# Branch gates and branch projections with tokens in rows, in a one-core hybrid layer in fp32

## The chip, the core and the metric

The kernel runs on one of the eight cores of a Trainium2 chip. The metric is the device time of one execution in microseconds (us), the median of several runs. The profile is one execution taken by the hardware profiler. Its engines: PE (TensorE, matmuls), PEld (its weight loads, which overlap PE), DVE (VectorE), ACT (ScalarE), POOL (GpSimd) and SP, whose queue issues most transfers.

## The reference, cut to what matters

One layer with 256 tokens of width 2048 (`D_MODEL`), all in fp32, and a final norm. Four branches of width 1024 (block attention A, convolution C, sparse attention S, attention into a memory M) are made from one projection of the normalised tokens:

```python
xn = rms_norm(x, ln_g)
(a_q, a_k, a_v, a_g, c_b, c_c, c_h, c_g, s_q, s_k, s_v, s_g, m_q, m_g,
 i_q, i_k, i_w, r_a, r_c, r_s, r_m) = [xn @ w for w in cols]
...                                     # y_a, y_c, y_s, y_m: [256, 1024] each, times silu of its gate
mem_n = rms_norm(mem, mem_ln_g)         # 256 memory tokens
mk, mv = jnp.split(mem_n @ w_mem_kv, 2, axis=-1)
...
merged = (jax.nn.sigmoid(r_a) * (y_a @ w_branch[0]) + jax.nn.sigmoid(r_c) * (y_c @ w_branch[1])
          + jax.nn.sigmoid(r_s) * (y_s @ w_branch[2]) + jax.nn.sigmoid(r_m) * (y_m @ w_branch[3]))
return rms_norm(x + merged @ w_out, final_g)
```

The branch gates r_a to r_m are 2048 wide each, 2048 inputs to a column; the branch products have 1024 inputs and 2048 columns.

## The kernel before, in words

**Products in parts.** Every fp32 operand of a large product is split exactly into hi and lo of 12 bits (`split`, L90 to L92: a cast on ACT, a subtraction on DVE), and three of the four partial products are summed in PSUM. Weights come from HBM in tiles "raw" of 1 MB, from a ring of three slots (L50) that `square_sums` (L168) and `load_mem` (L440) use too; `split_weights` (L101) splits each tile in two halves of 128x1024 into a ring of four (L51). A half is 2.8 us of PE's work.

**Two forms.** `project_t` (L127) makes the result transposed, columns on partitions: the weights are stationary, and for each chunk of 128 inputs and 128 columns there is one matmul with hi against the 2 x 256 columns of the tokens' hi and lo (L124, 512 columns) and one with lo against the tokens' hi (L125, 256). Its two halves are added by `sum_t` (L137: a copy on ACT, an addition on DVE) and scaled by 1/rms of each token, a row (`x_row`). `project` (L143) makes it with tokens in rows: the tokens are stationary, three matmuls of 512 columns (L161 to L163) for each half of the tokens.

**Where each is used.** Transposed: all q, k and gates of the branches (sections M_Q, M_G, S_Q, ... of 1024 columns), the branch gates (`gates`, L370, eight blocks of 256 columns for each branch, sigmoid at L378) and the branch products (`merge`, L381), which multiplies by the sigmoids and adds to `merged`, transposed too. In rows: the values (`to_values`, L213) and the output projection (L530), whose stationary operand is `mt`, the parts of `merged`; mt takes the place of x_hl, the parts of x (L508).

**Order.** M_Q (its first 512 columns while x arrives, L400), squares of x and x_row (L433 to L436), M_G with `load_mem` 0 to 3 hooked in after its four blocks (memT twice, mem twice, L452), w_mem_k, w_mem_v, memory attention, the indexer's projections, gates and products of M; then for S and A: q, k, values, gate section, attention over 8 heads (`masked_attention`, L248), gates, products; then C, and the output projection. x itself stays unnormalised in x_hl. Each engine works through its list in order; the lists are laid out by a planner that gives an instruction that comes earlier in the program the first turn and lets later ones pass when it isn't ready, so attention runs with the gates' matmuls in between. PSUM has eight banks: two tiles of two banks for projections, two for scores, one each for pp (transposed probabilities) and yp (L55 to L57).

Of the kernel before, what the change touches and what calls it, by code (L numbers as in the profile page):

```python
# [8 lines left out]
F32 = mybir.dt.float32  # L9
# [5 lines left out]
P = 128  # L15
# [17 lines left out]
# the columns of w_in that are projected transposed, in blocks of TB, and the place of each section's first block  # L33
SECTIONS = [(c, W) for c in (A_Q, A_K, A_G, C_B, C_C, C_H, C_G, S_Q, S_K, S_G, M_Q, M_G)] + [(R_0, 4 * D)]
# [3 lines left out]
BR_A, BR_C, BR_S, BR_M = 0, 1, 2, 3  # L38
TOPK = 64
# [3 lines left out]
def hybrid_kernel(ctx, tc, x, xT, mem, memT, ln_g, mem_ln_g, w_t, w_v, w_idx, conv_w, conv_b, w_mem_k, w_mem_v,  # L43
# [26 lines left out]
    # the tensor engine's clock and the activation table are ready when the first operands arrive  # L70
# [5 lines left out]
    wp = ps_1.tile([P, 512], F32, name="pp", tag="pp")  # L76
# [4 lines left out]
    # additive causal mask: columns 0:128 for queries 0..127, 128:384 for queries 128..255  # L81
# [19 lines left out]
    def split_weights(src, w):  # L101
        """(hi, lo, k) of each chunk k of the weights src [P, chunks, columns], in tiles w wide."""
# [11 lines left out]
    def split_tokens(raw, k, g, dst):  # L114
        """dst = (hi, lo) of raw * g."""
# [6 lines left out]
    def products_t(o, hi, lo, k, nk, act):  # L122
        """o[:, 0] + o[:, 1] gains chunk k of nk for the columns in hi, lo."""
        nc.tensor.matmul(o, lhsT=hi, rhs=act(k), start=(k == 0), stop=False)  # L124
        nc.tensor.matmul(o[:, 1], lhsT=lo, rhs=act(k)[:, 0], start=False, stop=(k == nk - 1))  # L125

    def project_t(src, act):  # L127
        """(a @ src)^T, at most TB columns: chunk j of 128 columns is acc[:, j, 0] + acc[:, j, 1]."""
        acc = ps_acc.tile([P, 2, 2, T], F32, name="acc", tag="acc")
        nk, c = src.shape[1:]  # L130
        for hi, lo, k in split_weights(src, TB):
            for j, c0 in enumerate(range(0, c, P)):
                c1 = min(c0 + P, c)
                products_t(acc[:c1 - c0, j], hi[:, c0:c1], lo[:, c0:c1], k, nk, act)
        return acc

    def sum_t(dst, acc, n=2, rows=P):  # L137
        """dst = both parts of project_t's result"""
        low = tmp.tile([P, 2, T], F32, name="low")
        nc.scalar.copy(out=low[:rows, :n], in_=acc[:rows, :n, 1])  # L140
        nc.vector.tensor_add(dst, acc[:rows, :n, 0], low[:rows, :n])

    def project(src, act, t_outer=False):  # L143
        """a @ src: acc[:, t, :c] for the tokens of half t."""
        nk, c = src.shape[1:]
        if t_outer:
            acc = [ps_s.tile([P, NB], F32, name=f"acc{t}", tag="s") for t in range(2)]
        else:
            both = ps_acc.tile([P, 2, NB], F32, name="acc", tag="acc")
            acc = [both[:, t] for t in range(2)]  # L150
        parts = split_weights(src, c)
        if t_outer:
            parts = list(parts)
            steps = ((p, t) for t in range(2) for p in parts)
        else:
            steps = ((p, t) for p in parts for t in range(2))
        for (hi, lo, k), t in steps:
            ts = slice(t * P, (t + 1) * P)
# [432 lines left out]
```

## Time and profile before

| | us |
|---|---|
| time, median of 3 runs | 1422.41 (1422.35 to 1422.84) |
| span of the profiled execution, first to last instruction | 1420.6 |
| PE busy | 1411.7 (99%) |
| PEld busy | 1223.6 (86%) |
| DVE busy | 902.0 (63%) |
| ACT busy | 724.5 (51%) |

The span leaves out what lies before the first and after the last instruction, 1.8 us against the median. Busy times are read with care: matmuls are pipelined and a matmul's busy time overlaps its neighbour's, so that a busy PE says only that it had something in work. Mean granted clock of the core: 0.998 of full speed.

### The profile page before, as it was taken

Reading aid. Unit: us, or ns where it says so; the run is one execution under the profiler, and the core shown is the slowest. Engines: PE = TensorE matmul, PEld = TensorE weight load, DVE = VectorE, ACT = ScalarE, POOL = GpSimd, SP = SyncE. Lnnn points to the kernel's source line nnn. Section 1 sums busy time; section 2 is a strip of 40 time slices with the busy share of each in tenths; the row PEclk is TensorE's granted clock in tenths of the full one; section 3 lists DMA queues with packets and bytes.
Section 4 is the critical chain, followed back from the end, with each engine's and each line's share of the span. In section 5 each row is a group of like instructions: output and inputs, shape, how many; then the busy total and the mean of one; then the engine's idle time right before and its main releaser. Section 6 shows DMA issues by size and latency. Waiting matters only on the chain.

```text
span 1420.6 us, 19646 instructions
## 1 busy us (share of the span) xinstructions
PE 1411.7 (99%) x7904; PEld 1223.6 (86%) x7904; DVE 902.0 (63%) x1169; ACT 724.5 (51%) x964; POOL 10.7 (1%) x25
## 2 busy tenths in 40 slices
PE   9999999999999999999999999999999999999997
PEld 8888888888888888888888888888888888888887
DVE  7755566658755558757655557857657656557754
ACT  7664356544444348744444347844444445445543
POOL 1000000000000000000000000000000000000000
PEclk9999999999999999999999999999999999999999
DMA  9775554555555554455555555455555666555552
GB/s 316 281 268 195 187 164 153 171 185 178 178 186 200 180 188 165 150 180 189 194 178 185 201 178 177 149 179 181 187 196 178 214 224 213 182 189 195 178 198 99
DMA packets 49963, 269.38 MB, mean 190 GB/s; under 512 B 6656, under 2 KB 17456, under 8 KB 19024
## 3 DMA queue, kind: packets, MB, share of 16 engines
q1 hardware_dynamic: 48960, 264.03, 54.7%
q0 software_dynamic: 624, 3.31, 0.6%
q8 instruction: 62, 1.02, 0.3%
q10 hardware_dynamic: 288, 0.79, 0.1%
q14 instruction: 29, 0.24, 0.0%
HBM read 265.88 MB, written 2.10 MB: 189 GB/s over the span
## 4 chain that ended last, share of the span: by engine, by line
PE 99%; issue 0%; DMA 0%; DVE 0%; ACT 0%; POOLq 0%; POOL 0%; DVEq 0%; SPq 0%; ACTq 0%
PE acc L124 53%; PE acc L125 27%; PE acc L163 5%; PE acc L162 5%; PE acc L161 5%; PE first L124 1%; PE pp L269 0%; PE s L242 0%; PE yp L242 0%; PE first L125 0%; PE yp L241 0%; PE s L241 0%; PE s L240 0%; PE yp L240 0%; PE s L254 0%
## 5 line engine op out<-in xcount | busy, mean ns | idle before, releaser
L124 PE MATMUL acc<-x_hl,hi 128*128 128x512 f32 x2576 | 917.5, 398 | 0.1
L92 DVE TENSOR_TENSOR lo<-raw,hi 128x1024 fp32r<-128x1024 f32 (+1 forms) x496 | 595.1, 1201 | 471.9 <-ACT hi L91 469.7
L91 ACT CAST hi<-raw 128x1024 fp32r<-128x1024 f32 (+1 forms) x496 | 511.1, 1031 | 655.4 <-PE acc L124 491.4
L125 PE MATMUL acc<-x_hl,lo 128*128 128x256 f32 x2576 | 725.4, 282 | 0.0
L124 PEld LDWEIGHTS acc<-x_hl,hi 128*128 128x128 f32 x2576 | 483.7, 188 | 114.9 <-DVE x_hl L118 0.8
L125 PEld LDWEIGHTS acc<-x_hl,lo 128*128 128x128 f32 x2576 | 483.1, 188 | 1.5
L124 PE MATMUL acc<-y,hi 128*128 128x512 f32 x512 | 181.2, 399 | 0.0
L125 PE MATMUL acc<-y,lo 128*128 128x256 f32 x512 | 143.7, 281 | 0.0
L124 PEld LDWEIGHTS acc<-y,hi 128*128 128x128 f32 x512 | 96.2, 188 | 23.6
L125 PEld LDWEIGHTS acc<-y,lo 128*128 128x128 f32 x512 | 96.7, 189 | 0.1
L140 ACT COPY low<-acc 128x512 f32<-128x512 f32 (+1 forms) x117 | 67.6, 578 | 0.3 <-PE acc L125 0.3
L161 PE MATMUL acc<-hi,mt 128*128 128x512 f32 (+1 forms) x160 | 55.5, 348 | 0.0
L163 PE MATMUL acc<-hi,mt 128*128 128x512 f32 (+1 forms) x160 | 55.3, 347 | 0.0
L162 PE MATMUL acc<-lo,mt 128*128 128x512 f32 (+1 forms) x160 | 55.0, 345 | 0.0
L163 PE MATMUL acc<-hi,x_hl 128*128 128x512 f32 x128 | 50.4, 394 | 0.0
L162 PE MATMUL acc<-lo,x_hl 128*128 128x512 f32 x128 | 50.2, 392 | 0.0
L161 PE MATMUL acc<-hi,x_hl 128*128 128x512 f32 x128 | 49.7, 388 | 0.0
L163 PEld LDWEIGHTS acc<-hi,mt 128*128 128x128 f32 x160 | 29.9, 187 | 4.2
L162 PEld LDWEIGHTS acc<-lo,mt 128*128 128x128 f32 x160 | 30.0, 188 | 4.0
L161 PEld LDWEIGHTS acc<-hi,mt 128*128 128x128 f32 x160 | 30.0, 188 | 3.6
L162 PEld LDWEIGHTS acc<-lo,x_hl 128*128 128x128 f32 x128 | 24.0, 188 | 5.5
L161 PEld LDWEIGHTS acc<-hi,x_hl 128*128 128x128 f32 x128 | 24.0, 188 | 5.4
(182 smaller groups left out, 980.4 us busy)
## 6 DMA issues: line engine op xcount, KB each, us to landing
raw<-in_w_t SPq DMA_DIRECT2D x156, 1024.0 KB, 5.2
raw<-in_w_branch SPq DMA_DIRECT2D x32, 1024.0 KB, 4.8
raw<-in_w_v SPq DMA_DIRECT2D x16, 1024.0 KB, 4.7
raw<-in_w_out SPq DMA_DIRECT2D x16, 1024.0 KB, 4.7
raw<-in_w_mem_k SPq DMA_DIRECT2D x8, 1024.0 KB, 5.1
raw<-in_w_mem_v SPq DMA_DIRECT2D x8, 1024.0 KB, 4.8
raw<-in_w_t SPq DMA_DIRECT2D x16, 256.0 KB, 5.8
raw<-in_x SPq DMA_DIRECT2D x2, 1024.0 KB, 4.8
```

Of the source, the lines that this page charges most:

```text
L91: nc.scalar.copy(out=hi, in_=src)
L92: nc.vector.tensor_sub(out=lo, in0=src, in1=hi.bitcast(F32))
L124: nc.tensor.matmul(o, lhsT=hi, rhs=act(k), start=(k == 0), stop=False)
L125: nc.tensor.matmul(o[:, 1], lhsT=lo, rhs=act(k)[:, 0], start=False, stop=(k == nk - 1))
L140: nc.scalar.copy(out=low[:rows, :n], in_=acc[:rows, :n, 1])
L161: nc.tensor.matmul(o, lhsT=ah, rhs=hi, start=(k == 0), stop=False)
L162: nc.tensor.matmul(o, lhsT=ah, rhs=lo, start=False, stop=False)
L163: nc.tensor.matmul(o, lhsT=al, rhs=hi, start=False, stop=(k == nk - 1))
```

## The change

Six things, all in one edit:

- The branch gates and the branch products are made in rows. `merge_branch` takes half of a branch's 2048 columns at a time: gates of two blocks of 512 columns (`project` with two sources in turn, four chunks each), sigmoid straight from PSUM, then the products of the same two blocks from y, times the sigmoids, added to merged. The order of one branch is gates, products, gates, products. The weights in HBM are laid out to suit.
- `merged` lies with tokens in rows. After the last branch `parts_of` transposes it on PE, 4 chunks x 2 token halves for each block of 512, into banks pp, and splits into mt.
- The tokens are normalised once: `normalize(b)`, hooked in after the four blocks of w_mem_k, adds the parts of four chunks of x_hl, multiplies by x_row and splits them back in place, through a tile xn from the ring raw. The later scalings by x_row or x_col go; M_Q and the memory's keys and values keep theirs.
- M_G moves behind the memory's values; `load_mem` moves ahead: 0 and 1 into the last two blocks of M_Q, 2 and 3 behind the squares of x.
- One ring of eight PSUM banks takes the place of the three pools.
- `sum_t` works bank by bank, 256 columns at a time.

```diff
-    ps_acc = ctx.enter_context(tc.tile_pool(name="ps_acc", bufs=2, space=PS))
-    ps_s = ctx.enter_context(tc.tile_pool(name="ps_s", bufs=2, space=PS))
-    ps_1 = ctx.enter_context(tc.tile_pool(name="ps_1", bufs=1, space=PS))
+    banks = ctx.enter_context(tc.tile_pool(name="banks", bufs=8, space=PS))
+    def bank(name):
+        return banks.tile([P, NB], F32, name=name, tag="b")
...
+    def sum_t(dst, acc, row=None, rows=P):
+        for j, a in enumerate(acc):
+            low = tmp.tile([P, T], F32, name="low")
+            nc.scalar.copy(out=low[:rows], in_=a[:rows, 1])
+            nc.vector.tensor_add(dst[:, j], a[:rows, 0], low[:rows])
+            if row is not None:
+                nc.vector.tensor_mul(dst[:, j], dst[:, j], row[:rows])
...
+    def project(srcs, act, name, t_outer=False):
+        nk = srcs[0].shape[1]
+        acc = [[bank(name)[:, :src.shape[2]] for src in srcs] for t in range(2)]
+        parts = [split_weights(src, src.shape[2]) for src in srcs]
...
+            steps = ((p, t, n) for k0 in range(0, nk, 4) for n in range(len(srcs))
+                     for p in itertools.islice(parts[n], 4) for t in range(2))
+        for (hi, lo, k), t, n in steps:
+            a = act(k)[:, :, t * P:(t + 1) * P]
+            products(acc[t][n], a[:, 0], a[:, 1], hi, lo, k == 0, k == nk - 1)
...
-    def gates(b):
-        sig = big.tile([P, KC, T], F32, name="sig", tag="m16b")
-        for j in range(8):
-            acc = project_t(w_t[FIRST[R_0] + 8 * b + j], x_act)
-            s = sig[:, 2 * j:2 * j + 2]
-            sum_t(s, acc)
-            nc.vector.tensor_mul(s, s, rows(x_row, 2))
-            nc.scalar.activation(out=s, in_=s, func=AF.Sigmoid)
-        return sig
...
+    def merge_branch(b, y, after=None):
...
+        for j in range(2):
+            blocks = (2 * j, 2 * j + 1)
+            sig = big.tile([P, 2, W], F32, name="sig", tag="m16b")
+            acc = project([w_n[GATES + 4 * b + n] for n in blocks], x_act, "r")
+            for t in range(2):
+                for n in range(2):
+                    nc.scalar.activation(out=sig[:, t, n * NB:(n + 1) * NB], in_=acc[t][n], func=AF.Sigmoid)
+            acc = project([w_branch[b, n] for n in blocks], lambda k: y[:, k], "w")
+            for n in range(2):
+                for t in range(2):
+                    m = merged[:, t, blocks[n] * NB:(blocks[n] + 1) * NB]
+                    g = sig[:, t, n * NB:(n + 1) * NB]
+                    if first:
+                        nc.vector.tensor_mul(m, acc[t][n], g)
+                    else:
+                        nc.vector.tensor_mul(g, acc[t][n], g)
+                        nc.vector.tensor_add(m, m, g)
+                if after is not None:
+                    after(blocks[n], merged)
...
+    for b in range(2, 4):
+        acc = project_t(w_sec(M_Q)[b], x_act)
+        load_mem(b - 2)
+        sum_t(q[:, 2 * b:2 * b + 2], acc)
+    for t in range(2):
+        square_sums(x, t, x_ss)
+    x_col, x_row = inv_rms(x_ss, "x")
+    nc.vector.tensor_mul(q, q, rows(x_row, 8))
+    for b in (2, 3):
+        load_mem(b)
     m_col, m_row = inv_rms(m_ss, "m")
+    def normalize(b):
+        ks = slice(4 * b, 4 * b + 4)
+        xn = rawp.tile([P, 4 * NB], F32, name="xn", tag="raw")[:, :4 * T].rearrange("p (k t) -> p k t", t=T)
+        nc.vector.tensor_add(xn, x_hl[:, ks, 0].bitcast(F32), x_hl[:, ks, 1].bitcast(F32))
+        nc.vector.tensor_mul(xn, xn, rows(x_row, 4))
+        split(x_hl[:, ks, 0], x_hl[:, ks, 1], xn)
+    k = to_heads("kt", w_mem_k, m_act, m_row, normalize)
+    v = to_values([w_mem_v[0], w_mem_v[1]], m_act, m_col)
+    gt = to_gate(M_G)
     y = memory_attention(q, k, v, gt)
     idx = indexer_parts()
-    sig = gates(BR_M)
-    merge(BR_M, sig, y)
+    merge_branch(BR_M, y)
...
+    def parts_of(n, merged):
+        for c in range(4 * n, 4 * n + 4, 2):
+            pp = halves(bank("pp"))
+            for i in range(2):
+                for t in range(2):
+                    nc.tensor.transpose(pp[:, i, t * P:(t + 1) * P], merged[:, t, (c + i) * P:(c + i + 1) * P], ident)
+            split(mt[:, c:c + 2, 0], mt[:, c:c + 2, 1], pp)
+    merge_branch(BR_C, y, after=parts_of)
```

## Rows read from the trace of the kernel before

**Rows 1.** The page: busy us of each engine; the chain that ended last, by engine.
```profile
PE 1411.7 (99%) x7904; PEld 1223.6 (86%) x7904; DVE 902.0 (63%) x1169; ACT 724.5 (51%) x964; POOL 10.7 (1%) x25
...
PE 99%; issue 0%; DMA 0%; DVE 0%; ACT 0%; POOLq 0%; POOL 0%; DVEq 0%; SPq 0%; ACTq 0%
```

**Rows 2.** Waits of PE, whole span: line, releaser, us in total, times, longest.
```profile
PE pp L78 <- DVE table L74: 1.2, 1, 1.2
```

**Rows 3.** Timeline of PE (start us, us, instruction): ends of M_Q and of pure stretches.
```profile
51.06 0.38 PE L179 MATMUL pr<-ident,x_col 128*128 128x128 f32 x2
...
444.15 0.39 PE L161 MATMUL acc<-hi,x_hl 128*128 128x512 f32 x1
...
488.10 0.39 PE L124 MATMUL acc<-x_hl,hi 128*128 128x512 f32 x1
...
1007.67 0.40 PE L124 MATMUL acc<-x_hl,hi 128*128 128x512 f32 x1
...
1279.03 0.39 PE L124 MATMUL acc<-y,hi 128*128 128x512 f32 x1
...
1324.24 0.40 PE L161 MATMUL acc<-hi,mt 128*128 128x512 f32 x1
```

**Rows 4.** Timeline of PE around four transposes in the memory attention.
```profile
196.02 0.60 PE L306 MATMUL pp<-ident,pr 128*128 128x128 f32 x4
196.38 0.36 PE L125 MATMUL acc<-x_hl,lo 128*128 128x256 f32 x1
```

**Rows 5.** Timeline of SP's queue: when tiles raw were issued after the first columns.
```profile
16.90 2.41 SPq L107 DMA_DIRECT2D raw<-in_w_t  x2
...
23.32 0.33 SPq L107 DMA_DIRECT2D raw<-in_w_t  x1
...
29.16 0.33 SPq L107 DMA_DIRECT2D raw<-in_w_t  x1
...
32.35 0.33 SPq L169 DMA_DIRECT2D raw<-in_x  x1
...
39.99 0.33 SPq L107 DMA_DIRECT2D raw<-in_w_t  x1
```

**Rows 6.** Transfers by name: count, KB each, median us from issue to landing.
```profile
raw<-in_x SPq DMA_DIRECT2D x2, 1024.0 KB, 4.8
```

**Rows 7.** Timeline of ACT: a square of x; five splits of a memT tile.
```profile
37.97 1.91 ACT L170 ACTIVATE raw<-raw 128x2048 f32<-128x2048 f32 x1
...
51.37 2.11 ACT L117 ACTIVATE m16a<-raw,g_m 128x256 fp32r<-128x256 f32 x5 [1.39 <-DMA raw<-in_memT]
```

**Rows 8.** Groups by line and shape, whole span: xcount | busy us, mean ns | idle before.
```profile
L92 DVE TENSOR_TENSOR lo<-raw,hi 128x1024 fp32r<-128x1024 f32 x476 | 582.4, 1225 | 462.9 <-ACT hi L91 461.0 <-PE acc L125 0.8
...
L91 ACT CAST hi<-raw 128x1024 fp32r<-128x1024 f32 x476 | 499.5, 1050 | 645.5 <-PE acc L124 484.6 <-PE acc L163 115.8 <-issue 21.8
```

**Rows 9.** Windows: us, busy of PE, PEld, DVE, ACT, POOL, granted clock, DMA.
```profile
96.70:142.00 45.30, 45.30 (x259) 39.38 (x258) 26.21 (x28) 20.53 (x24) 0.00 (x0) 1.00 0.57 195
186.00:270.00 84.00, 84.00 (x518) 74.11 (x517) 57.19 (x92) 53.90 (x87) 1.10 (x2) 1.00 0.52 168
533.50:601.50 68.00, 68.00 (x424) 60.73 (x424) 53.93 (x112) 57.03 (x112) 0.00 (x0) 1.00 0.49 160
1413.00:1417.00 4.00, 0.00 (x0) 0.00 (x0) 1.98 (x5) 1.44 (x3) 0.66 (x1) 0.85 0.44 165
1417.00:1420.60 3.60, 0.00 (x0) 0.00 (x0) 0.00 (x0) 0.00 (x0) 0.00 (x0) 0.50 0.58 224
```

**Rows 10.** Groups of PE by line in 533.3 to 601.7, the attention of S.
```profile
L124 PE MATMUL acc<-x_hl,hi 128*128 128x512 f32 x162 | 59.8, 402 | 0.0
```

**Rows 11.** Groups of ACT by line in 533.5 to 601.5.
```profile
L262 ACT ACT_TABLE_LOAD x5 | 6.4, 1283 | 0.2
L378 ACT ACT_TABLE_LOAD x4 | 5.1, 1283 | 0.1
```

**Rows 12.** Timeline of DVE behind the last head of S.
```profile
604.05 0.68 DVE L92 TENSOR_TENSOR y<-yt,y 128x512 fp32r<-128x512 f32 x1
```

More of the change, by code (lines that the diff above doesn't have):

```diff
@@ L1 @@
+import itertools
 from contextlib import ExitStack
@@ L32 @@
 R_0 = 14 * W + N_IDX
-SECTIONS = [(c, W) for c in (A_Q, A_K, A_G, C_B, C_C, C_H, C_G, S_Q, S_K, S_G, M_Q, M_G)] + [(R_0, 4 * D)]
+SECTIONS = [(c, W) for c in (A_Q, A_K, A_G, C_B, C_C, C_H, C_G, S_Q, S_K, S_G, M_Q, M_G)]
 FIRST = {}
@@ L127, in project_t @@
     def project_t(src, act):
-        acc = ps_acc.tile([P, 2, 2, T], F32, name="acc", tag="acc")
         nk, c = src.shape[1:]
+        acc = [halves(bank("acc")) for _ in range(0, c, P)]
         for hi, lo, k in split_weights(src, TB):
@@ L164, in project @@
-        return acc if t_outer else both
+            held = list(parts[0])
+            steps = ((p, t, 0) for t in range(2) for p in held)
+        else:
+            steps = ((p, t, n) for k0 in range(0, nk, 4) for n in range(len(srcs))
[3 more added lines that the diff above has]
+            products(acc[t][n], a[:, 0], a[:, 1], hi, lo, k == 0, k == nk - 1)
+        return acc
@@ L274, in masked_attention @@
             if h % 2 == 0:
-                yp = ps_1.tile([P, 2, T], F32, name="yp", tag="yp")
+                yp = halves(bank("yp"))
             hs = slice(h * P, (h + 1) * P)
@@ L287, in memory_attention @@
         for h in range(4):
-            s = ps_s.tile([P, 2, T], F32, name="s", tag="s")
+            s = halves(bank("s"))
             qk = [(in_parts(q[:, 2 * h + c]), in_parts(k[:, 2 * h + c])) for c in range(2)]
@@ L308, in memory_attention @@
             split(pt[:, 0], pt[:, 1], pp)
-            yp = ps_1.tile([P, 2, T], F32, name="yp", tag="yp")
+            yp = halves(bank("yp"))
             vm = [in_parts(v[:, m, h * 256:(h + 1) * 256]) for m in range(2)]
@@ L400, in first_columns @@
     def first_columns(c0, dst):
         src = w_t[FIRST[c0]:FIRST[c0] + 2].rearrange("b p k c -> p k b c")
-        acc = ps_acc.tile([P, 2, 2, T], F32, name="acc", tag="acc")
-        outs = [acc[:, 0], acc[:, 1]] + [ps_s.tile([P, 2, T], F32, name="first", tag="s") for _ in range(2)]
+        outs = [halves(bank("first")) for _ in range(4)]
         xraw = big.tile([P, KC, T], F32, name="xraw", tag="m16b")
@@ L429, in hybrid_kernel @@
     first_columns(M_Q, q)
-    for b in range(2, 4):
-        acc = project_t(w_sec(M_Q)[b], x_act)
-        sum_t(q[:, 2 * b:2 * b + 2], acc)
-    for t in range(2):
-        square_sums(x, t, x_ss)
-    x_col, x_row = inv_rms(x_ss, "x")
-    nc.vector.tensor_mul(q, q, rows(x_row, 8))
     m_hl = [big.tile([P, 8, 2, T], F32R, name=n, tag=n) for n in ("m16a", "m16b")]
@@ L505, in hybrid_kernel @@
         split(y[:, s, 0], y[:, s, 1], bt[:, s])
-    sig = gates(BR_C)
     mt = big.tile([P, KC, 2, T], F32R, name="mt", tag="xhl")
-    def parts_of(js, merged):
-        split(mt[:, js, 0], mt[:, js, 1], merged[:, js])
-    merge(BR_C, sig, y, after=parts_of)
+    def parts_of(n, merged):
+        for c in range(4 * n, 4 * n + 4, 2):
+            pp = halves(bank("pp"))
+            for i in range(2):
+                for t in range(2):
+                    nc.tensor.transpose(pp[:, i, t * P:(t + 1) * P], merged[:, t, (c + i) * P:(c + i + 1) * P], ident)
+            split(mt[:, c:c + 2, 0], mt[:, c:c + 2, 1], pp)
+    merge_branch(BR_C, y, after=parts_of)
     xr = [big.tile([P, D], F32, name=f"xr{t}", tag=tag) for t, tag in ((0, "qt"), (1, "kt"))]
```

127 lines of the change are left out of this document (44 added, 83 removed).

## The prediction

> **What bounds the kernel now.** First the page's busy times and its chain of work: TensorE is busy 99% of the span and the chain is PE for 99% [rows 1]. Then the waits of PE: 1.2 us in the whole execution, all of it before the first real matmul [rows 2]. So every microsecond has a matmul in it, nobody is waited for, and time can only be won by making TensorE's own stream shorter; any new wait of PE is paid in full. VectorE (63%) and ScalarE (51%) are not the bound over the whole span [rows 1], but two stages come close, and they matter below. Busy times of matmuls overlap (pipelined), so I take no price from a mean duration but from distances between start times in the PE timeline, over stretches with nothing else in them.
>
> **The change, part by part.**
>
> *Gates and branch products in row form.* I call a unit 512 output columns times one chunk of 128 inputs times 256 tokens. Transposed it is four pairs (L124 with 512 columns, L125 with 256); in rows it is two triples (L161 to L163) of 512 columns. Both stream 3072 columns, with 8 and 6 instructions. S_V is a stretch of pure triples: 444.15 to 488.10, 43.95 us for 192 matmuls, 228.9 ns each, so 1.3734 us a unit (32 units). Pure pairs on x: 1007.67 to 1279.03, 271.36 us for 1536 matmuls = 192 units, 1.4133 us a unit. Pairs on y: 1279.03 to 1324.24, 45.21 us for 32 units, 1.4128 us [rows 3]. The change moves the gates, 4 branches x 4 blocks x 16 chunks = 256 units, and the branch products, 4 x 4 x 8 = 128 units. 256 x 0.0399 + 128 x 0.0394 = 10.2 + 5.0 = **-15.3 us**, all on the path. At the granted 2.4 GHz 3072 columns are 1280 ns, so both forms carry about 16 ns per instruction over their columns, and two instructions fewer is the gain.
>
> The Trainium skill, in "TensorE: Matmul & The Clock Gate", section "Back-to-back issue gap", gives the distance of matmuls in a stream as the columns at 2.4 GHz plus about 2.5 ns. This speaks against the change: with equal columns it leaves 384 x 2 x 2.5 ns = 1.9 us (an estimate from that page). The trace does not agree, with 228.9 ns where the rule has 215.8 [rows 3]; the rows decide.
>
> *Transposes of the merged result.* 16 chunks x 2 token halves = 32 new 128x128 matmuls. Four of the same kind at L306 hold PE for 0.36 us, 0.09 each [rows 4]: **+2.9 us**. They wait for VectorE's sums, but the schedule can run the output projection over chunks 0 to 7 meanwhile (8 units, 11 us), and of the last two blocks the first one's products end 5.5 us (4 units) before the second's. mt lies in x_hl's place, so the first half's splits wait until the last gates are done, 22 us of branch products ahead of their use. End: 0, at most 1.
>
> *No wait behind the merge.* sum_t, the row scaling and the sigmoid of the gates leave VectorE and ScalarE (several instructions of about 0.6 us for each block). PE waited for none of them [rows 2]: 0.
>
> *The start.* This is the step that costs. Before, memT (2 tiles) and mem (2 tiles) were loaded inside the M_G section, one per block of 11.3 us. Now there is no such section ahead of w_mem_k: between the last M_Q weights and the first w_mem_k weights SP issues memT, memT, x, x, mem, mem, all through the three slots of "raw" that the weights use, and w_mem_k's first product follows M_Q, whose end is marked by the transposes of x_col at 51.06 [rows 3]. Before, the slots were given out at 16.9 and about 19 (M_Q block 2), 23.32 and 29.16 (block 3), 32.35 (x), 39.99 (next weights) [rows 5]. A slot is held from issue to landing, 4.8 us for a full tile of x [rows 6], and then for its use: 1.91 us for a square, 8 x 0.43 for the splits of a memT tile [rows 7], plus a queue in front of ScalarE. Same working with the new order: block 2 at 16.9 and 19; memT at 23.3, free about 35; block 3 at 29.2 and 32.4, free about 37.7 and 42 (paced by PE); memT 35, free 44.5; x 37.7, free 46.5; x 42, free 49.1; mem 44.5; mem 46.5; first w_mem_k 49.1. It lands about 54; cast and subtraction, 1.05 and 1.2 us [rows 8], give the first product at 56.6 where PE is out of work at 51.1. No other matmul is ready: V comes after, M_G needs the normalised x, which needs x_row first. **+5.5 us** (0 if the tiles pass faster than I count, 8 if ScalarE's queue holds each tile one square longer). The tail shows that the granted clock falls from 2.4 GHz when PE is idle: 0.85 in the first 4 us after the last matmul, 0.50 (1.2 GHz) in the next 3.6 [rows 9]. So a gap of 5 us may be followed by slow matmuls: **+1.0** (0 to 2).
>
> *Normalising in place.* Four times an addition, a multiplication, a cast and a subtraction over 128x1024: 3 x 1.2 = 3.7 us of VectorE each, 14.7 in all [rows 8], in w_mem_k's stretch. VectorE is busy there 26.2 of 45.3 us [rows 9]; with 14.7, two 2 us leftovers (the scaling of q, the copies) and finer sums it stands at some 90 to 100%. Weights are split up to four halves (11 us of PE) ahead, but after the gap that store is empty: **+0.5** (0 to 3). Each xn also borrows a slot of raw; the two left turn over in about 10 us each and PE needs a tile in 5.7, so weights still keep up, barely. M_G is 44 us later: no wait. In exchange the scalings of every later section go, off the path.
>
> *Less cover for attention.* In the masked branches attention begins when the gate section S_G (A_G) is done and ran beside the gates: 533.5 to 601.5, with 162 pairs of gates in it [rows 9, 10], 57 us, the other 11 being attention's own. Now the gates come in two halves: 32 units = 44 us, then the first half's branch products, whose weights hold the four split buffers until y is there, so that the second half's gates can't pass them. Of those products the first 8 units (11 us) need y of heads 0 to 3 only. 44 + 11 + 11 = 66 us of work for 68 us of attention. But attention gets faster: of ScalarE's 57.0 busy us of 68.0 [rows 9], 9 loads of activation tables by Exp and Sigmoid taking turns are 11.5 us [rows 11]; the sigmoids now come in two bunches after 39 us or so, and the copies of sum_t go. The last y was split at 604.05 [rows 12], 3 us after the window. Memory branch: 84 us of window [rows 9]; idx 17 (48 pairs), gates 44, 11 and its own 12 are 84 too. **+0.5** in each of three branches, 1.5 (0 to 12).
>
> *PSUM.* Gates and branch products hold four banks each of eight; attention had four of its own before and now shares. A block's gates end 5.5 us before its neighbour's, so its banks come free by two sigmoids before the products want them: 0. The convolution branch has y early: 0.
>
> Sum: -15.3 + 2.9 + 5.5 + 1.0 + 0.5 + 1.5 = **-3.9 us**. The profiled execution spans 1420.6, and the median of the runs is 1422.41, 1.8 of it outside the span, which stays: 1422.4 - 3.9 = **1418.5 us**.
>
> **Rivals.**
> 1. *The start is hidden.* For: tiles that PE doesn't pace may pass a slot in 7 us, and the count above adds up queues that may not meet. Against: three slots, six extra tiles and one ScalarE queue. Then 5.5 + 1.0 go: 1412 us.
> 2. *Attention is uncovered* (slower). If a head's share of VectorE and ScalarE doesn't shrink, or the products wait for the whole y, PE runs dry once attention takes longer than 66 us; with the 11 us of products useless 13 us are lost in each masked branch and as much in the memory branch at the worst, half of it typical: 1418.5 + 10 to 35, about 1432. It decides from about 2.5 us per branch on (three times that, and the 1.5 taken, eat up the gain). For: covers equal to within 2 us. Against: ScalarE's table loads, and that PE never waited in these windows.
> 3. *The page's rule holds and nothing is gained per matmul:* 1418.5 + 15.3 - 1.9, by rows the same with the pairs' and triples' pace equal: about 1433. The S_V rows are this very form, on this very operand, so I give it little.
> 4. *The one ring does what it should not:* a bank is given out in program order only, gates wait for all of attention's banks, and 3 x 50 us of cover go: 1570. No row shows a ring shared in this way.
>
> **How the numbers follow.** Forecast (1415 to 1424) 0.50, start hidden 0.24, attention uncovered 0.20, rule 0.02, ring 0.04. About 0.2% (2.8 us) is what a measurement of this kernel can tell from no change: faster is below 1419.6, slower above 1425.3. Faster: 0.24 and six tenths of the forecast's case, 0.54. Same: the other four tenths and a little of case 2, 0.23. Slower: 0.23. Range: from 1410 (all unknown costs at their lower ends: 1422.4 - 15.3 + 2.9) to 1430 (start 8 + 2, normalising 3, attention 7).
>
> **What the profile would show.** Gates and products as triples at 229 ns from start to start, 44 us for 32 units; 32 transposes of 0.09; a wait of PE of about 5 us near 51 on ScalarE or VectorE after a landing of w_mem_k, its first issue near 49; a granted clock below 1 just after; PE waits of 0 to 2 us where a branch's first products meet the last heads. Wrong if pairs' time doesn't fall by 15 us, if the w_mem_k weights are issued before 44, or if PE waits over 3 us within an attention.

## The result, and the profile after

| | before | after |
|---|---|---|
| time, median of 4 runs (us) | 1422.4 (1422.35 to 1422.84) | 1531.1 (1529.15 to 1532.43) |
| span of the profiled execution | 1420.6 | 1528.7 |
| mean granted clock of TensorE | 0.998 | 0.954 |

The changed kernel takes 1.0762 times as long (95% interval 1.0747 to 1.0778): 108.7 us slower, where 3.9 us faster was forecast and the range ended at 1430. The page of the kernel after, its first part (busy time, share of the span, count), its slices (busy tenths; granted clock in tenths) and the chain that ended last, to set beside [rows 1]:

```profile
span 1528.7 us, 18000 instructions
...
PE 1447.9 (95%) x7168; PEld 1219.8 (80%) x7168; DVE 834.8 (55%) x1087; ACT 689.6 (45%) x948; POOL 11.7 (1%) x25
...
PE   9799957999999996899999997799999999999998
...
PEclk9899977999999996899999998699999999999999
...
PE 91%; DVE 4%; ACT 3%; issue 1%; DMA 1%; POOLq 0%; POOL 0%; DVEq 0%; ACTq 0%; SPq 0%
```

In the slices PE has four weak places: the second slice (the start), the sixth and seventh (M), the sixteenth and seventeenth (S), the twenty-fifth and twenty-sixth (A). The three later ones are the three attentions. The granted clock falls in the same slices. PE has fewer matmuls than before, 7168 where there were 7904 (384 units with two fewer each, and 32 transposes), and VectorE and ScalarE do less than before; the time went into waits. The waits of PE, longest sums first (us in total, times, longest), where before showed 1.2 us in all [rows 2]:

```profile
PE pp L280 <- DVE pr L277: 25.4, 10, 4.2
PE pp L317 <- DVE pr L313: 16.7, 4, 5.9
PE yp L251 <- ACT pt L99: 11.8, 18, 1.2
PE pr L189 <- POOL m_col L185: 6.3, 1, 6.3
```

PE waits inside attention: its transposes of the probabilities (pp) for the softmax on VectorE, its products with the values (yp) for the transposed probabilities. Nothing else fills the time. The timeline of PE in S shows it (start, duration, line, operation, tiles, in brackets the idle time before and who ended it). The first stretch is where attention begins, the second where it ends:

```profile
580.34 0.38 PE L265 MATMUL s<-kt,qt 128*128 128x128 f32 x2
...
585.24 0.81 PE L280 MATMUL pp<-ident,pr 128*128 128x128 f32 x3 [4.16 <-DVE pr L277]
587.25 0.58 PE L251 MATMUL yp<-pt,part 128*128 128x256 f32 x1 [1.21 <-ACT pt L99]
587.63 0.63 PE L265 MATMUL s<-kt,qt 128*128 128x128 f32 x2
...
623.59 0.45 PE L280 MATMUL pp<-ident,pr 128*128 128x128 f32 x1 [1.81 <-DVE pr L277]
623.69 0.78 PE L156 MATMUL r<-hi,x_hl 128*128 128x512 f32 x1
624.26 0.63 PE L157 MATMUL r<-lo,x_hl 128*128 128x512 f32 x1
```

Two things are to be seen. The second tile of scores starts at 587.63, right behind the first matmul of yp at 587.25, and 7.3 us after the first tile, while PE stands idle for 4.16 and 1.21 us. And the first matmul of the gates (tile r, L156) starts at 623.69, 0.10 us behind the first of the three transposes into the last pp, the tile that the program asks for just ahead of r. Between 580.3 and 623.7 not one matmul of the gates runs, though x_hl had been ready all along. Before, 162 pairs of gates ran inside the attention of S [rows 10]. The windows of the three attentions (start and end, length, then busy us and count of PE, PEld, DVE, ACT, POOL, granted clock, DMA share, GB/s), to set beside [rows 9]:

```profile
198.00:243.70 45.70, 23.59 (x103) 19.54 (x102) 21.39 (x53) 18.96 (x48) 0.00 (x0) 0.59 0.07 23
580.30:623.70 43.40, 24.87 (x100) 19.88 (x98) 28.11 (x84) 25.41 (x76) 0.00 (x0) 0.56 0.09 32
937.00:980.50 43.50, 25.04 (x100) 20.09 (x99) 28.11 (x84) 25.34 (x76) 0.11 (x1) 0.54 0.09 32
```

Some 100 matmuls in each, hardly any transfer, and a granted clock of 0.54 to 0.59. That is 132.6 us in which PE does attention alone; the prediction put attention's own matmuls at 11 us in a masked branch and 12 in M, 34 in all. So by that count about 99 us are lost there, the larger part of the 108.7. The stages, from the boundaries in the two timelines (us):

| stage | before | after | difference |
|---|---|---|---|
| start of the span to the end of M_G, memory keys and values | 186.0 | 198.0 | +12.0 |
| M, attention to branch products | 168.0 | 200.2 | +32.2 |
| S, the same | 147.3 | 177.2 | +29.9 |
| A, the same | 147.5 | 177.8 | +30.3 |
| C | 316.5 | 314.9 | -1.6 |
| output projection and norm | 88.8 | 91.3 | +2.5 |

They hold 105.3 of the 108.1 us by which the span grew. The three branches with an attention take 30 to 32 us more each, the start 12. C, which has no attention, shows the sign that was forecast: its gates and products are 96 units, 3.8 us by [rows 3], against which stand 16 of the transposes and a wait of 0.6 for merged (L525); the other 16 transposes and a wait of 0.7 are the +2.5 of the output projection.

### The profile page after: what moved, and what is told of

It reads as the page before. It is cut to its first block, busy times and chain, and to the rows that moved or that the text cites. A ratio compares the mean times of both kernels' runs of the same rounds, so it can differ in the third digit from the quotient of the medians.

```text
span 1528.7 us, 18000 instructions
## 1 busy us (share of the span) xinstructions
PE 1447.9 (95%) x7168; PEld 1219.8 (80%) x7168; DVE 834.8 (55%) x1087; ACT 689.6 (45%) x948; POOL 11.7 (1%) x25
## 4 chain that ended last, share of the span: by engine, by line
PE 91%; DVE 4%; ACT 3%; issue 1%; DMA 1%; POOLq 0%; POOL 0%; DVEq 0%; ACTq 0%; SPq 0%
PE acc L132 25%; PE acc L133 13%; PE r L157 8%; PE r L156 8%; PE r L158 8%; PE w L156 4%; PE w L157 4%; PE w L158 4%; PE v L158 3%; PE v L157 3%; PE v L156 3%; PE o L157 2%; PE o L156 2%; PE o L158 2%; PE first L132 1%
## 5 line engine op out<-in xcount | busy, mean ns | idle before, releaser
L132 PE MATMUL acc<-x_hl,hi 128*128 128x512 f32 x1520 | 538.9, 398 | 0.0
L133 PE MATMUL acc<-x_hl,lo 128*128 128x256 f32 x1520 | 427.4, 281 | 0.0
L132 PEld LDWEIGHTS acc<-x_hl,hi 128*128 128x128 f32 x1520 | 285.7, 188 | 71.1
L133 PEld LDWEIGHTS acc<-x_hl,lo 128*128 128x128 f32 x1520 | 285.4, 188 | 0.5
L157 PE MATMUL r<-lo,x_hl 128*128 128x512 f32 x512 | 202.4, 395 | 0.0
L156 PE MATMUL r<-hi,x_hl 128*128 128x512 f32 x512 | 202.4, 395 | 0.0
L158 PE MATMUL r<-hi,x_hl 128*128 128x512 f32 x512 | 201.3, 393 | 0.0
L156 PEld LDWEIGHTS r<-hi,x_hl 128*128 128x128 f32 x512 | 97.2, 190 | 21.7
L158 PEld LDWEIGHTS r<-hi,x_hl 128*128 128x128 f32 x512 | 96.9, 189 | 21.2
L158 PE MATMUL w<-hi,y 128*128 128x512 f32 x256 | 99.6, 389 | 0.0
L157 PE MATMUL w<-lo,y 128*128 128x512 f32 x256 | 99.6, 389 | 0.0
L156 PE MATMUL w<-hi,y 128*128 128x512 f32 x256 | 99.1, 389 | 0.0
L156 PEld LDWEIGHTS w<-hi,y 128*128 128x128 f32 x256 | 48.1, 188 | 10.0
L156 PE MATMUL o<-hi,mt 128*128 128x512 f32 (+1 forms) x160 | 55.4, 347 | 0.0
L158 PE MATMUL o<-hi,mt 128*128 128x512 f32 (+1 forms) x160 | 55.1, 346 | 0.0
```

The source lines that it names most:

```text
L156: nc.tensor.matmul(o, lhsT=ah, rhs=hi, start=start, stop=False)
L157: nc.tensor.matmul(o, lhsT=ah, rhs=lo, start=False, stop=False)
L158: nc.tensor.matmul(o, lhsT=al, rhs=hi, start=False, stop=stop)
```

## The experiments

Three theories for the 92 us of the attentions, as the expectations name them. **A**: the tiles of one ring get their banks in the order in which the program asks for them, so nothing that the program asks for behind attention can start before attention's last tile has. **B**: the ring is short of free banks, and a pair of gate blocks wants four at once. **C**: it isn't the banks at all; the gates in two halves, or the kernel's other edits, leave attention uncovered (rival 2). The times of before beside these runs were 1422.3 to 1422.7 us throughout.

### One ring put into the kernel before

The kernel before with nothing changed but its pools: one ring of four slots of two banks for everything.

```
-    ps_acc = ...tile_pool(name="ps_acc", bufs=2, space=PS)
-    ps_s = ...tile_pool(name="ps_s", bufs=2, space=PS)
-    ps_1 = ...tile_pool(name="ps_1", bufs=1, space=PS)
+    ps_acc = ps_s = ps_1 = ...tile_pool(name="banks", bufs=4, space=PS)
     ...                                   # every tile from it: tag="b"
```

> The kernel before with nothing changed but PSUM: its three pools become one ring of four slots of two banks, all tiles of PSUM taken from it. Theory A: the transposed gates wait for the last head too; each attention runs bare, 30 to 35 us lost in each of three branches, 1510 to 1530 us. Theory B and C: the gates need one slot at a time as before and all of them lie ahead of the products, so little changes, 1422 to 1435.

Measured: 1531.4 us (1530.31 to 1531.85), 1.0764 times before (1.0748 to 1.0780). The one edit costs as much as the whole change, 1.4 us above A's forecast and far above that of B and C. Its waits of PE, the window of the attention of S, and PE where that window ends:

```profile
PE pp L267 <- DVE pr L264: 26.5, 10, 4.8
PE pp L304 <- DVE pr L300: 15.8, 4, 4.9
PE yp L238 <- ACT pt L89: 11.0, 18, 0.9
```

```profile
572.60:616.10 43.50, 24.96 (x100) 19.98 (x98) 28.43 (x84) 25.45 (x75) 0.00 (x0) 0.55 0.10 35
```

```profile
615.99 0.44 PE L267 MATMUL pp<-ident,pr 128*128 128x128 f32 x1 [1.81 <-DVE pr L264]
616.09 0.78 PE L122 MATMUL acc<-x_hl,hi 128*128 128x512 f32 x1
```

These are the waits and the window of the kernel after, nearly number for number, and here too the first gate (acc, L122) starts 0.10 us behind the first transpose of the last pp, in a kernel with transposed gates, eight blocks of them in a row, and scalings by x_row. C falls as the cause of the attentions' loss. Four slots are fewer than the six tiles that the three pools gave, so this run alone doesn't tell the turn (A) from the room (B); the next one does.

### Gates one block at a time

The kernel after with gates that ask for two banks at once, not four.

```
-            acc = project([w_n[GATES + 4 * b + n] for n in blocks], x_act, "r")
-            for t in range(2):
-                for n in range(2):
-                    nc.scalar.activation(out=sig[:, t, n * NB:(n + 1) * NB], in_=acc[t][n], ...)
+            for n in range(2):
+                acc = project([w_n[GATES + 4 * b + blocks[n]]], x_act, "r")
+                for t in range(2):
+                    nc.scalar.activation(out=sig[:, t, n * NB:(n + 1) * NB], in_=acc[t][0], ...)
```

> The changed kernel, one ring of eight, with the gates of one block of 512 columns at a time, so that they need two banks at once instead of four. Theory B: with the demand halved the gates find banks beside attention's and most of the 100 us come back, 1430 to 1460. Theory A: the order of the ring is as it was, first gates right behind the last head's last bank, 1525 to 1540.

Measured: 1530.6 us (1530.22 to 1531.00), 1.0759 (1.0738 to 1.0781): no change. PE at the end of the attention of S:

```profile
622.90 0.45 PE L280 MATMUL pp<-ident,pr 128*128 128x128 f32 x1 [1.81 <-DVE pr L277]
623.00 0.78 PE L156 MATMUL r<-hi,x_hl 128*128 128x512 f32 x1
```

With half the demand the gates still start 0.10 us behind the first transpose into attention's last pp. B falls; it is the turn that they wait for, not the room. The Trainium skill, in "Perfetto Trace Analysis", section "Optimization Strategy", puts a bubble that repeats on the saturated engine down to PSUM or SBUF that may be too small for the next tile; this run speaks against that reading here.

### Two rings

The kernel after with two rings of four banks: "b" for projections, gates and products, "t" for attention, the indexer and the transposes.

```
-    banks = ctx.enter_context(tc.tile_pool(name="banks", bufs=8, space=PS))
-    def bank(name):
-        return banks.tile([P, NB], F32, name=name, tag="b")
+    banks = ctx.enter_context(tc.tile_pool(name="banks", bufs=4, space=PS))
+    def bank(name, tag="b"):
+        return banks.tile([P, NB], F32, name=name, tag=tag)
     ...
-            s = bank("s")[:, :384]
+            s = bank("s", "t")[:, :384]       # and pp, yp, lg, wp, pr
```

> The changed kernel with the eight banks in two rings of four instead of one of eight: projections, gates and products in one, what attention, indexer and transposes use in the other. Theory A (a ring hands its banks out in program order, so the gates' matmuls can't start before the last head has taken its last bank): the gates run inside the attentions again, the 34 us lost in each of three branches come back, 1424 to 1438 us, PE's waits on pp fall from 42 us to under 5. Theory C (what uncovers attention is that only half of a branch's gates lie ahead of products that need y): nothing changes but a few us, 1515 to 1535. Theory B (gates in rows need four banks at once and find too few free): also back to 1424 to 1438, since four are reserved; run e5_one_block tells it from A.

Measured: 1455.2 us (1454.64 to 1455.65), 1.0229 (1.0214 to 1.0244). Of the loss 75.9 us are gone, PE's waits on pp are down to 0.6 us, as A said, and the granted clock is back at 0.988; but the forecast of 1424 to 1438 was missed by 17. Part of A was right, and something was left. Its longest wait of PE, and PE in the attention of S:

```profile
PE w L156 <- ACT y L99: 10.4, 4, 3.6
```

```profile
555.00 0.39 PE L158 MATMUL r<-hi,x_hl 128*128 128x512 f32 x1
555.23 0.28 PE L251 MATMUL yp<-pt,part 128*128 128x256 f32 x1
555.35 0.38 PE L265 MATMUL s<-kt,qt 128*128 128x128 f32 x2
```

Gates now run inside attention (r at 555.00). But the next scores still come right behind the first matmul of yp, 0.12 us after it: attention's own tiles s, pp and yp still share a ring, so one head's scores wait for their turn behind the yp of the head before. Attention then lasts longer than its gates, and the branch products (w, L156) wait for y.

### The start as before

The kernel after with M_G ahead of the memory keys again, the loads of memory hooked into it; the tokens are still normalised in place, in the keys' stretch.

```
-        load_mem(b - 2)                       # in M_Q's last two blocks
-    for b in (2, 3):
-        load_mem(b)
+    gt = to_gate(M_G, x_row, load_mem)
     ...
-    gt = to_gate(M_G)                         # behind the memory's values
```

> The changed kernel with only the start's order put back: M_G ahead of the memory's keys with the loads of memT and mem hooked in after its blocks (scaled by x_row), normalising in place still in the stretch of the memory's keys. If the start costs what the two traces show (M_G, keys and values end at 198.0 instead of 186.0), 12 us come back: 1517 to 1522. If the loss lies in normalising in place rather than in the loads, PE still loses 3 us or more in the stretch of the keys and fewer than 8 us come back.

Measured: 1517.6 us (1517.33 to 1518.37), 1.0669 (1.0651 to 1.0687). Against the kernel after 13.5 us come back, a little more than the start's stage had lost (12.0). So the new start costs 13.5 here, and the normalising, which stayed where it was, leaves no cost to be seen.

### Two rings and the start as before

Both edits together.

> Both repairs: two rings of four banks, and the start's order put back; gates and products in rows, half a branch at a time, and normalising in place stay. Sum of the terms: 1422.4 - 15.3 (form) + 2.9 (transposes) + 0 to 12 (cover of attention by half the gates: 66 us of work for 68) = 1410 to 1422. Rival: a ring of four for gates and products that each take four banks stalls PE at every change between them, 1 to 3 us in 16 places: 1425 to 1450.

Measured: 1443.5 us (1441.62 to 1444.56), 1.0145 (1.0131 to 1.0159). The start gives 11.8 more, but the kernel is still 21 us behind the one before: the sum of the terms (1410 to 1422) was missed, and the time lies in the range of the rival that the expectation names, a ring of four that stalls PE at every change between gates and products. In its profile PE's longest wait is still that of the branch products for y, 10.8 us in four. Attention in S lasts 85 us here, from 531 to 616, against 68 before [rows 9]. What holds it up could be the shared ring of attention's tiles (theory **D**), the half gates after all (**C** again, on this smaller loss), or that rival.

### Attention's banks told apart

The same, with attention's four banks divided as before: two for scores, one for pp, one for yp.

```
-        return banks.tile([P, NB], F32, name=name, tag=tag)
+        return banks.tile([P, NB], F32, name=name, tag=tag, bufs={"b": 4, "t": 2, "pp": 1, "yp": 1}[tag])
     ...
-            pp = bank("pp", "t")[:, :384]
+            pp = bank("pp", "pp")[:, :384]
-                yp = halves(bank("yp", "t"))
+                yp = halves(bank("yp", "yp"))
```

> e4_two_rings_start with attention's ring of four split up as before the change: two banks for scores, one for pp, one for yp. In e4 each masked branch still takes 16 us more than 147.3 - 3.7 us, and attention spreads over 85 us instead of 68. Theory D (the shared ring of four makes a head's tiles wait for each other's order, which slows attention): attention is back at 68 us and the loss at 0 to 4 us a branch, 1412 to 1422 us. Theory C (half a branch's gates plus the first products are too little work for attention): it stays within 3 us of 16 in each of the two, 1434 to 1446.

Measured: 1413.4 us (1413.16 to 1414.53), 0.9939 (0.9924 to 0.9953): 30.1 us from this edit alone, and faster than before. No bank was added; the same four are handed out in three queues, not in one. PE where attention begins in S, and the window of S:

```profile
531.16 0.38 PE L265 MATMUL s<-kt,qt 128*128 128x128 f32 x2
...
531.75 0.38 PE L265 MATMUL s<-kt,qt 128*128 128x128 f32 x2
531.89 0.48 PE L156 MATMUL r<-hi,x_hl 128*128 128x512 f32 x1
```

```profile
531.30:602.30 71.00, 71.00 (x364) 59.97 (x363) 51.32 (x106) 53.31 (x107) 0.00 (x0) 1.00 0.46 156
```

Scores of two tiles start 0.59 us apart (587.63 - 580.34 = 7.29 in the kernel after), a gate follows at once, and PE is busy through all 71 us at full clock. Of PE's waits (2.5 us in all) 0.7 for y are left, where two rings had 10.4. D holds, and C falls here too; so does the rival, for gates and products still share their ring of four.

### All gates ahead of the products

The same, with the four gate blocks of a branch made first and the products behind them, so that attention has 88 us of gates beside it, not 44 and the first products.

```
+        sig = big.tile([P, 2, D], F32, name="sig", tag="m16b")
         for j in range(2):
             blocks = (2 * j, 2 * j + 1)
-            sig = big.tile([P, 2, W], F32, name="sig", tag="m16b")
             ...                               # gates of the two blocks
+        for j in range(2):
+            blocks = (2 * j, 2 * j + 1)
             ...                               # products of the two blocks
```

> e8_attention_pools with all gates of a branch ahead of its products, as before the change; gates and products in rows, projections' ring of four, normalising in place stay. Theory C: 1409 to 1414, the full cover of 90 us is back. Theory D: no further gain over e8 beyond 2 us. If it stays above 1418 under both, changing over between gates and products on one ring of four, or normalising in place, costs what is left.

Measured: 1411.8 us (1411.59 to 1411.98), 0.9926 (0.9909 to 0.9942), 1.6 us less than with half gates. The runs of the two kernels don't overlap. This is the price of halving the gates.

### The form alone

The kernel before with its pools, start, order of sections and scalings; only gates and branch products in rows, all gates first, and the merged result transposed on PE.

```
-        for j in range(8):
-            acc = project_t(w_t[FIRST[R_0] + 8 * b + j], x_act)
-            ...                               # sum_t, times x_row, sigmoid
+        for n in range(4):
+            acc = project(w_v[4 + 4 * b + n], x_act)
+            for t in range(2):
+                nc.scalar.activation(out=sig[:, t, n * NB:(n + 1) * NB], in_=acc[:, t], func=AF.Sigmoid,
+                                     scale=x_col[:, t:t + 1])
```

> The kernel before with only the form changed: gates and branch products in rows, all gates of a branch ahead of its products, the sigmoid scaled by x_col, merged transposed on PE; pools, start and scalings as before. If the triples hold 229 ns and nothing waits: 1422.4 - 15.3 + 2.9 = 1410, at most 1412. If the rule of equal columns held, 1423 to 1426.

Measured: 1411.35 us (1410.81 to 1411.47), 0.9920 (0.9906 to 0.9934), 11.3 us faster than before and the fastest of all. Busy times from its page, and all its waits of PE:

```profile
PE 1400.0 (99%) x7168; PEld 1188.3 (84%) x7168; DVE 844.7 (60%) x1073; ACT 689.9 (49%) x896; POOL 10.6 (1%) x25
```

```profile
PE pp L78 <- DVE table L74: 1.2, 1, 1.2
PE acc L124 <- DVE x_hl L118: 0.3, 1, 0.3
```

PE waits 1.5 us in all, so the 11.3 us are PE's own stream made shorter. The transposes in that stream (PE, inside the output projection):

```profile
1319.60 0.40 PE L161 MATMUL acc<-hi,mt 128*128 128x512 f32 x1
1319.84 0.82 PE L514 MATMUL mtp<-ident,merged 128*128 128x128 f32 x6
1320.41 0.48 PE L162 MATMUL acc<-lo,mt 128*128 128x512 f32 x1
1320.73 0.39 PE L163 MATMUL acc<-hi,mt 128*128 128x512 f32 x1
```

### The pools alone

The kernel after with only its banks divided as in "Attention's banks told apart": 4, 2, 1 and 1.

> The changed kernel with nothing undone but the one ring: four banks for projections, gates and products, two for scores, one for pp, one for yp, as e8_attention_pools has them; the changed start stays. The rings' share of the loss is the distance from the changed kernel's 1531.1. By e8 (1413.4) plus the start's 12 us (two traces): 1424 to 1427. If rings and start hide each other: under 1420.

Measured: 1423.6 us (1422.53 to 1424.32), 1.0007 (0.9997 to 1.0016), just under the 1424 to 1427 that were expected. One edit to the ring takes 107.5 us off the changed kernel and leaves the time of before. Set against the run with the old start (1413.4), the new start costs 10.2 us in this kernel.

### Two memory tiles later

The same, with the last two loads of memory (mem, for its squares) and m_row behind the first block of the memory keys, so that they hold neither a slot of "raw" nor ScalarE's queue ahead of the first weights. **E**: the six tiles in three slots are the cause; **F**: the queues of ScalarE and VectorE in that stretch, or normalising in place, are.

```
-    for b in (2, 3):
-        load_mem(b)
-    m_col, m_row = inv_rms(m_ss, "m")
-    k = to_heads("kt", w_mem_k, m_act, m_row, normalize)
+    for b in range(4):
+        acc = project_t(w_mem_k[b], m_act)
+        if b == 0:
+            for i in (2, 3):
+                load_mem(i)
+            m_col, m_row = inv_rms(m_ss, "m")
+        normalize(b)
+        sum_t(k[:, 2 * b:2 * b + 2], acc, m_row)
```

> e11_pools_only with the two squares of mem and m_row moved behind the first block of the memory's keys, so that the first w_mem_k tile gets its slot of raw two tiles earlier (issue near 45.6 instead of 51.8 us). Theory E (the start's loss is the slots: six extra tiles in three slots): first product near 54 to 56 instead of 60, 5 to 8 us less than e11. Theory F (ScalarE's and VectorE's queues in that stretch, or normalising in place): under 2 us less.

Measured: 1419.1 us (1417.65 to 1421.27), 0.9976 (0.9967 to 0.9986), 4.5 us less than with the pools alone: more than F's bound of 2, less than the 5 to 8 of E. First its SP queue (the issue of w_mem_k), then PE around it:

```profile
46.64 0.94 SPq L115 DMA_DIRECT2D raw<-in_w_mem_k  x2
50.18 0.33 SPq L179 DMA_DIRECT2D raw<-in_mem  x1
```

```profile
51.99 0.38 PE L189 MATMUL pr<-ident,x_col 128*128 128x128 f32 x2
52.93 0.50 PE L132 MATMUL acc<-m16a,hi 128*128 128x512 f32 x1 [0.56 <-ACT hi L99]
```

In the kernel after, the same queue and PE:

```profile
35.90 0.33 SPq L438 DMA_DIRECT2D raw<-in_memT  x1
38.18 4.29 SPq L179 DMA_DIRECT2D raw<-in_x  x2
45.63 2.12 SPq L179 DMA_DIRECT2D raw<-in_mem  x2
51.77 0.33 SPq L115 DMA_DIRECT2D raw<-in_w_mem_k  x1
```

```profile
52.81 0.43 PE L189 MATMUL pr<-ident,x_col 128*128 128x128 f32 x2 [1.68 <-POOL x_col L185]
59.55 0.69 PE L189 MATMUL pr<-ident,m_col 128*128 128x128 f32 x2 [6.31 <-POOL m_col L185]
59.89 0.78 PE L132 MATMUL acc<-m16a,hi 128*128 128x512 f32 x1
```

The run is to be set beside the pools alone, where the first weights were issued and the first product ran so:

```profile
50.13 3.93 SPq L115 DMA_DIRECT2D raw<-in_w_mem_k  x2
```

```profile
59.24 1.20 PE L132 MATMUL acc<-m16a,hi 128*128 128x512 f32 x2
```

Two tiles fewer ahead of the weights bring their issue 3.5 us forward (50.13 to 46.64) and the first product 6.3 (59.24 to 52.93). The 2.8 beyond the issue are more than the slots give by themselves: the same edit takes the squares of mem out of ScalarE's queue ahead of the first cast, and the transposes of m_col out of PE's list ahead of the first product. So it doesn't tell E from F. Of the 6.3 us only 4.5 reach the end, and 5.7 of the start's 10.2 stay (1419.1 - 1413.4). The trace shows where most of these go: PE now waits four times for hi or lo of the keys' weights, 3.7 us in all, in a stretch (52 to 70) in which VectorE is busy for 16.4 of 18 us, at a granted clock of 1.00 throughout. That is what F names, and it counts once the slots are out of the way. The other 2 us stay open.

### The account

Medians, each step the difference of two runs:

| step | from | us |
|---|---|---|
| before | | 1422.6 |
| gates and products in rows, transposes | form alone | -11.3 |
| finer sums, normalising in place | all gates first, less form alone | +0.5 |
| gates in two halves | told apart, less all gates first | +1.6 |
| M_G moved, memory loaded ahead | pools alone, less told apart | +10.2 |
| attention's own tiles in one ring | two rings, less pools alone | +31.6 |
| gates and products in attention's ring | after, less two rings | +75.9 |
| after | | 1531.1 |

The steps hang on the order in which they are taken: the start is 13.5, 11.8 or 10.2 by the kernel in which it is put back. The +0.5 also holds the projections of two blocks in turn, and it is about what the kernel before moved from one set of runs to another (1422.3 to 1422.7), so it isn't clear of zero.

## Why the prediction was wrong, point by point

**PSUM: the step that failed.** It says of the shared ring that attention had four banks before and now shares, and prices that at 0, because it counted when banks come free. It is 107.5 us, and the prediction's own sign of being wrong was there, waits of PE of 4.2 and 5.9 us within an attention. The room in the banks didn't matter (one block at a time: no change); the order did (the same four banks in three queues: 30.1 us). The paragraph on the order of work had the reason in hand: PE runs gates inside attention because the planner lets a later instruction pass one that isn't ready. A tile that must wait its turn in a ring can't pass. Told as what the traces show: with a shared ring a tile begins right behind the first matmul of the tile asked for before it (587.63 behind 587.25; 623.69 behind 623.59; 555.35 behind 555.23), and with banks for each role two tiles of scores start 0.59 us apart. That the turn is given when PE's list is laid out, and not on the chip, is argued from the kernel, not shown.

**Rival 4** had this very mechanism, a bank given out in program order only, and 0.04 for it, on the ground that no row shows a ring shared in this way. That is a reason for a wide bound, not for a small chance: an unknown of 0 to 150 us on three attentions stayed out of a range that took in the bounds of the other unknown costs. Its price was too high: 3 x 50 us taken; for each some 33 measured in the windows (98.6 in three), 36 by the pools alone (107.5 in three). All its cover did go, 57 us of gates in S. But bare attention needs only 43.4 us, not 68, since its tiles no longer share PE with gates; 43.4 less its own 11 is 32, and the stages of S and A grew by 30. The rival also saw only the gates; that attention's own heads take turns as well (31.6 us) was in no part of the text.

**Form.** Forecast -15.3 and +2.9, together -12.4; form alone measured -11.3 (by its interval 9.4 to 13.4 faster). The triples kept their pace on x: in the trace of the form alone the gates of C, 384 matmuls, run from 1177.48 to 1265.37, 228.9 ns each as in [rows 3]. The transposes were a little under-sized: six hold PE for 0.57 us, and the matmul behind them starts its successor 0.32 later in place of 0.23, so 0.11 each and 3.5 in all, where [rows 4] gave 0.09. The rest, 0.5, is less than these runs can tell. Rival 3 is out: with the pairs' and triples' pace equal the form alone would have been at 1422.6 + 2.9 = 1425.5. The section of the Trainium skill behind it ("TensorE: Matmul & The Clock Gate", "Back-to-back issue gap") calls its formula, 216 ns at 512 columns, the gap of an isolated matmul, and gives 131 ns for a stream in which each matmul has its weight load, which is what these streams are. The prediction applied the formula to the stream. Neither figure agrees with the 228.9 ns here; the measured distances do.

**The start.** The mechanism was right in outline (the last run doesn't tell the slots from the queues of ScalarE and VectorE): six extra tiles through three slots, PE out of work near 51, a wait of some 5 us, a lower clock behind it. The sizes were not: 5.5 + 1.0 forecast, 8 + 2 as the bound, 10.2 to 13.5 measured (by the kernel in which it is undone). The working of the slots slipped by a little at each tile: memT at 35.90 for 35, x at 38.18 and 42.1 for 37.7 and 42, mem at 45.63 and 47.4 for 44.5 and 46.5, the weights at 51.77 for 49.1, and the first product at 59.89 for 56.6. PE's wait in front of it is put down to m_col on GpSimd, whose transposes stand ahead of the product in PE's list; the forecast followed the weights and never asked when m_col would be ready. It cost little: ScalarE's first cast of the weights ran from 58.08 and takes 1.05, so without m_col the product would have started near 59.1. And the clock term was 1.0 where the trace has more: see the last section. "Wrong if the weights are issued before 44" named only the error to the good side.

**Rival 1**, the start hidden, is out by the same rows.

**Normalising in place.** 0.5 forecast (0 to 3). The start as before kept it and still got all of its stage's loss back, and in the kernel after PE's only wait behind the first product of the keys is 0.5 us for a lo from VectorE. As far as these rows go it is right; in the last run, with the weights earlier, the queues of ScalarE and VectorE show in 3.7 us of waits, and the normalising's part in them isn't told apart.

**Less cover for attention, rival 2.** 1.5 forecast for the halves, 1.6 measured once the rings are apart; with bounds of 0 to 12 a match this close is luck. So the halves do just cover attention, as was counted (66 us of work for 68). Rival 2's time of 1432 was not what happened either. This right count hid the wrong one: cover was reckoned as work that is there, not as work that is allowed to start.

**No wait behind the merge; the end.** The form alone waits for none of it (1.5 us of waits in all, none of them there), nor do the pools alone. In the kernel after the transposes wait 1.3 us for merged (0.6 and 0.7), a little over the bound of 1. Right but for that.

**As a whole.** With the ring's banks told apart the changed kernel stands at 1423.6, inside the range; against that the forecast is 5.1 us too low, of which the start is 3.7 (10.2 for 6.5) and the form 1.1. It was one term, taken for nothing, that put the time 101 us outside.

## What to carry to other kernels

Before several uses are put into one ring of buffers, write down the order in which the program asks for its tiles and look for a tile that waits for another engine; whatever comes behind it in that ring loses its right to run ahead, and a trace that shows later work inside such a wait (gates inside attention) gives the price. Count cover as work that may start, not as work that exists. And an edit that no row of the trace shows belongs in the range with its worst end, above all where a rival has already named the mechanism.

## What the runs showed of the hardware

The loss of an uncovered attention is larger than its idle time. In the window of S in the kernel after PE sits idle for 43.40 - 24.87 = 18.5 us, and its own 100 matmuls, about 11 us of work between gates (68 less 57, [rows 9, 10]), keep it busy for 24.9, at a mean granted clock of 0.56, between the two levels of 1.2 and 2.4 GHz (0.50 and 1.0). How much of this is the clock and how much the ends of matmuls that no successor overlaps isn't told apart. The first matmul behind attention takes 0.78 us and its successor starts 0.57 us later (623.69 to 624.26), where a triple's distance is 0.229 at full clock.

The same shows at the start. The two windows around the gap:

```profile
51.00:60.00 9.00, 1.02 (x7) 0.65 (x5) 5.91 (x9) 7.52 (x11) 2.33 (x2) 0.80 0.85 330
60.00:70.00 10.00, 9.50 (x39) 7.70 (x38) 9.66 (x10) 4.84 (x6) 0.00 (x0) 0.67 0.56 210
```

PE is busy for 1.0 us of the first nine, and in the ten that follow, with PE busy for 9.5, the granted clock is 0.67 on average; the first 32 matmuls of the keys take 9.25 us (59.89 to 69.14) where 16 pairs take 5.65 at the pace of [rows 3]: 3.6 us, of which 0.5 is a wait. PE in that stretch:

```profile
62.19 0.63 PE L132 MATMUL acc<-m16a,hi 128*128 128x512 f32 x1
62.62 0.41 PE L133 MATMUL acc<-m16a,lo 128*128 128x256 f32 x1
62.83 0.63 PE L132 MATMUL acc<-m16a,hi 128*128 128x512 f32 x1
```

A pair takes 0.64 us here, from start to start, in place of 0.353. So 3.1 us of lower pace followed a gap of 6 to 7 us, where the tail of the kernel before [rows 9] had suggested about one.
